# A gate product in seven block products instead of eight, in the last stage of a two-layer decoder trunk

## Chip, cores and metric

The kernel runs on one core of a Trainium2 chip. The time is the device time of one execution in microseconds (us). The median of three runs before the change is 1260.3 us (1259.97 to 1260.51). One further execution was profiled.

## What is computed

Two decoder layers over 512 tokens of width 1024, all in f32. Layer 0 mixes by sliding-window attention and a short convolution, layer 1 by chunked gated linear attention. Each layer then adds a gated MLP with a width-3 causal convolution, and a per-layer embedding. The change touches the end of layer 1: the down projection of its MLP, and the embedding that closes the kernel.

```python
for i in range(DEPTH):
    ...
    x = x + _conv_ffn(_rms_norm(x, ffn_norm[i]), ffn_w_up[i], ffn_conv_w[i], ffn_conv_b[i], ffn_w_down[i])
    x = x + _per_layer_embedding(x, p[i], ple_norm[i], ple_w_gate[i], ple_w_proj[i])
...
def _per_layer_embedding(x, p_i, norm, w_gate, w_proj):
    gate = jax.nn.sigmoid(_rms_norm(x, norm) @ w_gate)     # 512x1024 @ 1024x1024
    return gate * (p_i @ w_proj)                           # 512x256 @ 256x1024
```

## The kernel before

**Numbers.** The matmuls take operands of type fp32r. Every operand is split into a high part (ScalarE copies it to fp32r) and a low part (VectorE subtracts the high part from the original): `split` (L92) for activations, `cut` (L114) for weights. `mm3` (L149) then issues three matmuls for each block: high by high, high by low, low by high. So a product over a contraction of 1024 takes 8 blocks of 128 with 3 matmuls each, per 128 output rows and 512 output columns.

**Data.** The residual stream lies transposed in SBUF: eight tiles `xT[m]` of 128 channels by 512 tokens. The normalisation is deferred. `advance` (L228) multiplies a finished `xT[m]` by the gain, splits it, and adds its squares to `acc`; `end_norm` (L242) sums `acc` over the channels with four small matmuls, and `rsqrt` (L157) gives one factor per token, which is applied after the product.

**Weights.** A weight tile comes in by one DMA of up to 1 MB on SyncE's queue into one of two buffers `raw`, and is cut into halves that rotate through three buffers each of `wh` and `wl`. A DMA waits for the cuts of the tile before the last, a cut waits for the matmuls that read the same buffer three cuts earlier.

**The down projection** (`project`, L274) makes two output tiles m, m+1 at a time: 22 contraction blocks by 3 matmuls by 2 tiles, 132 matmuls a pair, four pairs. After each tile, `done` (L298) adds it to `xT[m]` and calls `advance`.

**The last stage** (`ple1`, L770) takes the eight split tiles as stationary operand, 128 tokens at a time, and the gate weights as moving operand, 512 columns at a time. First the left 512 columns for all four token tiles t, over all eight k, into four PSUM banks `ps`. Then p is transposed and split (`load_p`, L713), `back` (L787) transposes all of x back into eight tiles `xt`, and for each t `finish` (L798) closes the left half and the right half follows: 24 matmuls, then `finish` again. `finish` makes the product of p with the projection weights (six matmuls into `pj`), the sigmoid of the gate product (ScalarE), multiplies by `pj`, adds `xt` (both VectorE) and stores the result. The last right half is made in two pieces of 256 columns.

**Order.** A scheduler places the instructions of every engine at build time by priority and its own estimate of time, and assigns the waits between engines; at run time every engine goes through its list in order, and a waiting instruction holds up all that stand behind it. SyncE's list holds the DMAs. SBUF is given out by pools: the memory of the MLP's pool goes to the last stage's pool when the MLP's tiles have been read for the last time.

## Time and profile before

| | |
|---|---|
| median of 3 runs | 1260.3 us |
| the profiled execution: time | 1260.71 us |
| its span, first to last instruction | 1258.8 us |
| TensorE (PE) busy | 1244.9 us, 99% |
| VectorE (DVE) busy | 772.7 us, 61% |
| ScalarE (ACT) busy | 541.1 us, 43% |
| DMA, over the span | 117.42 MB, 93 GB/s |
| last stage, from its first matmul to the end of the span | 1194.48 to 1258.8 us |

All stretches of time below are in microseconds from the start of the span. PE is TensorE's matmul, PEld its weight load, POOL is GpSimd, SP is SyncE. A row of the timeline gives the start, the duration, the engine, the line of the kernel, the operation and its tiles; in brackets stands how long the engine had been idle before, and what ended that. Matmuls overlap: one of 512 columns is shown with 0.39 us, but the next starts 0.23 us later, and it is this step from start to start that counts. The same holds, by less, for VectorE and ScalarE.

### The profile page before, as it was taken

To read this page: it belongs to the slowest core of one execution; us is meant where nothing else is said; L and a number is where in the kernel's file an instruction comes from. 1 tells how busy PE (TensorE), PEld (TensorE's weight loads), DVE (VectorE), ACT (ScalarE), POOL (GpSimd) and SP (SyncE) were. 2 spreads that over 40 slices of the span, in tenths; PEclk is the share of its full clock that TensorE was granted. 3 is DMA by queue.
4 is the path that set the end of the run, shared out by engine and by line. 5 is a ranking of instruction groups with operands and counts; after the bars stand their busy time and mean duration, and the time that the engine had idled before them with its cause. 6 is when DMAs were issued, how large, how long until landed. Compare 5 with 4: busy or idle time off the path is not lost.

```text
span 1258.8 us, 14853 instructions
## 1 busy us (share of the span) xinstructions
PE 1244.9 (99%) x5851; PEld 1038.1 (82%) x5851; DVE 772.7 (61%) x1190; ACT 541.1 (43%) x831; POOL 54.1 (4%) x150
## 2 busy tenths in 40 slices
PE   7999999999999999999999999999999999999998
PEld 7777788888888888888989988888888888888887
DVE  6776566777777633346679765557777777433343
ACT  6456344444444422234563544335444444232341
POOL 2500000000000000000100000000000000000000
PEclk9999999999999999999999999999999999999999
DMA  6221232333332233223322222333222233222331
GB/s 212 73 76 55 79 99 93 100 101 101 100 100 92 76 111 99 92 74 101 109 89 67 68 68 67 100 100 102 98 88 86 98 100 101 92 92 93 108 107 61
DMA packets 110473, 117.42 MB, mean 93 GB/s; under 512 B 2712, under 2 KB 105682, under 8 KB 110404
## 3 DMA queue, kind: packets, MB, share of 16 engines
q1 hardware_dynamic: 108512, 114.83, 28.0%
q10 hardware_dynamic: 1332, 1.23, 0.3%
q8 instruction: 46, 0.75, 0.2%
q0 software_dynamic: 560, 0.42, 0.2%
q14 instruction: 23, 0.19, 0.0%
HBM read 114.37 MB, written 2.10 MB: 93 GB/s over the span
## 4 chain that ended last, share of the span: by engine, by line
PE 92%; DVE 3%; ACT 2%; issue 1%; POOL 1%; DMA 1%; SPq 0%; DVEq 0%; POOLq 0%; ACTq 0%
PE ps L153 28%; PE ps L155 28%; PE ps L154 28%; PE pa L492 1%; PE pa L1001 1%; DMA xin<-in_x_dram 1%; PE pa L1115 1%; PE pa L154 1%; DVE wl L134 1%; PE pa L153 1%; PE pa L155 1%; PE pa L538 1%; PE pa L1092 0%; POOL rq L163 0%; PE pa L1117 0%
## 5 line engine op out<-in xcount | busy, mean ns | idle before, releaser
L133 ACT ACTIVATE wh<-raw 128x1024 fp32r<-128x1024 f32 (+4 forms) x222 | 224.7, 1015 | 384.5 <-PE ps L154 319.4
L134 DVE TENSOR_TENSOR wl<-raw,wh 128x1024 fp32r<-128x1024 f32 (+4 forms) x222 | 258.6, 1167 | 184.0 <-ACT wh L133 182.9
L153 PE MATMUL ps<-a,wh 128*128 128x512 f32 x864 | 337.4, 390 | 0.0
L154 PE MATMUL ps<-a,wh 128*128 128x512 f32 x864 | 337.0, 390 | 0.0
L155 PE MATMUL ps<-a,wl 128*128 128x512 f32 x864 | 336.8, 390 | 0.0
L153 PEld LDWEIGHTS ps<-a,wh 128*128 128x128 f32 x864 | 162.5, 188 | 34.3 <-issue 0.7
L155 PEld LDWEIGHTS ps<-a,wl 128*128 128x128 f32 x864 | 162.5, 188 | 34.0 <-issue 0.2
L154 PEld LDWEIGHTS ps<-a,wh 128*128 128x128 f32 x864 | 162.5, 188 | 33.8 <-issue 0.3
L682 DVE SCALAR_TENSOR_TENSOR zt<-z,vfa,zt 128x512 f32<-128x512 f32 x176 | 131.4, 749 | 3.6 <-ACT zt L680 0.6
L153 PE MATMUL ps<-b,wh 128*128 128x512 f32 x320 | 126.3, 396 | 0.6 <-ACT b L97 0.5
L155 PE MATMUL ps<-b,wl 128*128 128x512 f32 x320 | 125.3, 392 | 0.0
L154 PE MATMUL ps<-b,wh 128*128 128x512 f32 x320 | 124.9, 391 | 0.0
L679 DVE TENSOR_TENSOR z<-ps,R 128x512 f32<-128x512 f32 x88 | 60.4, 688 | 74.7 <-PE ps L155 74.7
L153 PE MATMUL ps<-ah,wh 128*128 128x512 f32 x224 | 87.1, 389 | 0.0
L154 PE MATMUL ps<-al,wh 128*128 128x512 f32 x224 | 87.1, 389 | 0.0
L155 PE MATMUL ps<-ah,wl 128*128 128x512 f32 x224 | 87.1, 389 | 0.0
L680 ACT ACTIVATE zt<-z,vfb 128x512 f32<-128x512 f32 x88 | 70.9, 807 | 5.0 <-DVE z L679 3.3
L153 PEld LDWEIGHTS ps<-b,wh 128*128 128x128 f32 x320 | 60.0, 188 | 14.0 <-ACT b L97 1.3
L155 PEld LDWEIGHTS ps<-b,wl 128*128 128x128 f32 x320 | 60.1, 188 | 12.5
L154 PEld LDWEIGHTS ps<-b,wh 128*128 128x128 f32 x320 | 60.1, 188 | 12.2
L704 ACT ACTIVATE zt<-zt 128x512 f32<-128x512 f32 x44 | 27.8, 631 | 74.8 <-DVE zt L682 74.8
L299 DVE TENSOR_TENSOR xT<-xT,ps 128x512 f32<-128x512 f32 x32 | 22.0, 688 | 57.4 <-PE ps L155 57.4
(290 smaller groups left out, 1506.1 us busy)
## 6 DMA issues: line engine op xcount, KB each, us to landing
raw<-in_ffn_w_up_dram SPq DMA_DIRECT2D x44, 1024.0 KB, 5.0
raw<-in_ffn_w_down_dram SPq DMA_DIRECT2D x16, 1024.0 KB, 5.1
raw<-in_hy_w_in_dram SPq DMA_DIRECT2D x8, 1024.0 KB, 5.0
raw<-in_ple_w_gate_dram SPq DMA_DIRECT2D x8, 1024.0 KB, 5.0
raw<-in_gla_w_in_dram SPq DMA_DIRECT2D x8, 1024.0 KB, 5.3
raw<-in_ffn_w_down_dram SPq DMA_DIRECT2D x8, 768.0 KB, 4.3
raw<-in_gla_w_out_dram SPq DMA_DIRECT2D x4, 1024.0 KB, 5.0
raw<-in_gla_w_in_dram SPq DMA_DIRECT2D x4, 672.0 KB, 4.0
```

Of the source, the lines that this page charges most:

```text
L133: nc.scalar.activation(hv, v, AF.Copy)
L134: nc.vector.tensor_tensor(lv, v, hv.bitcast(F32), ALU.subtract)
L153: mm(out, lh, rh, start=start, stop=False)
L154: mm(out, lh, rl, start=False, stop=False)
L155: mm(out, ll, rh, start=False, stop=stop)
L299: self.nc.vector.tensor_tensor(self.xT[m], self.xT[m], ps, ALU.add)
L492: nc.tensor.matmul(pb[:, hh * 256 : hh * 256 + w], qTs[t][64 * g : 64 * g + 64, hq, :], kT[64 * g : 64 * g + 64, k0 : k0 + w], start=True, ...
L538: nc.tensor.transpose(pb[:, hh * P : (hh + 1) * P], s[:, 4 * g + hh, c * P : (c + 1) * P], self.ident)
L679: nc.vector.tensor_tensor(z[:, 2:], ps, R, ALU.mult)
L680: nc.scalar.activation(y, z[:, 2:], AF.Identity, scale=w2[:, f : f + 1], bias=bb[:, f : f + 1])
L682: nc.vector.scalar_tensor_tensor(out=y, in0=z[:, tap : tap + S], scalar=w[:, f : f + 1], in1=y, op0=ALU.mult, op1=ALU.add)
L704: nc.scalar.activation(y, y, AF.Gelu)
```

## The change

The gate product of the last stage is written as a product of 2 by 2 blocks: the contraction in even and odd blocks of 128 (e and o), the tokens in a first and a second half (1 and 2), the columns in a left and a right half. Eight block products become seven by Strassen's method in Winograd's form. With b11, b21 the left weights of the even and odd blocks and b12, b22 the right ones, the products are e1 b11, o1 b21, s1 (b12-b11), s2 (b22-b12+b11), s3 (b22-b12), s4 b22 and o2 (b21-b22+b12-b11), with s1 = e2+o2, s2 = s1-e1, s3 = e1-e2, s4 = o1-s2.

- The sums and differences of the activations are made where the down projection of layer 1 finishes a tile (`blocks`): for each pair of tiles VectorE makes s1 to s4 from the two gained tiles, and four operands (e1, o, s1 with s2, s3 with s4) are split, in place of two.
- Those of the weights are made in the last stage (`minus`), each in two VectorE instructions of 128x1024; the resulting blocks are cut like the others (`chunk`).
- Partial products that several results share are copied from PSUM to SBUF (`keep`, ScalarE) and added later (`summed`, VectorE), or stay in their bank and are added to.
- The gate weights arrive as four blocks of 1 MB: b11 and b21 into the two `raw` buffers, b12 and b22 (`rawx`) into the last stage's pool. The projection weights (512 KB) have one buffer `wjr` and are loaded three times. p comes in two halves on SyncE's queue, during the MLP, instead of one DMA on ScalarE's.
- The projection matmuls of a result (`proj`) now stand ahead of its gate product, and the transposes `back` are spread over the stage.
- In the whole stage the order of PE, VectorE and ScalarE is that of the source (`manual_schedule`); SyncE's is still the scheduler's. Each of the 7 products is 24 matmuls; the last one is ordered by result tile, its second tile in two pieces of 256 columns.

```diff
...
+    def blocks(self, m, gain, scratch):
+        nc = self.nc
+        H = S // 2
+        tags = ("a0", "a1") if m < 4 else ("b0", "b1")
+        gx = scratch()
+        nc.scalar.activation(gx, self.xT[m], AF.Copy, scale=gain[:, m : m + 1])
+        def parts(x):
+            w = x.shape[1]
+            h, l = self.pair(self.fp, *tags)
+            self.split((h[:, :w], l[:, :w]), x)
+            return lambda b, c: (h[:, b * H + c * P : b * H + (c + 1) * P], l[:, b * H + c * P : b * H + (c + 1) * P])
+        if m % 2 == 0:
+            self.even = gx
+            self.e1 = parts(gx[:, :H])
+        else:
+            e, o = self.even, gx
+            op = parts(o)
+            s12, s34 = scratch(), scratch()
+            nc.vector.tensor_tensor(s12[:, :H], e[:, H:], o[:, H:], ALU.add)
+            nc.vector.tensor_tensor(s12[:, H:], s12[:, :H], e[:, :H], ALU.subtract)
+            s12p = parts(s12)
+            nc.vector.tensor_tensor(s34[:, :H], e[:, :H], e[:, H:], ALU.subtract)
+            nc.vector.tensor_tensor(s34[:, H:], o[:, :H], s12[:, H:], ALU.subtract)
+            s34p = parts(s34)
+            e1 = self.e1
+            at = lambda f, b: lambda c: f(b, c)
+            self.forms.append(
+                dict(e1=at(e1, 0), o1=at(op, 0), o2=at(op, 1), s1=at(s12p, 0), s2=at(s12p, 1), s3=at(s34p, 0),
+                     s4=at(s34p, 1))
+            )
+        self.squares(m)
...
@@ -707,19 +752,37 @@
                     nc.vector.tensor_tensor(y, g, y, ALU.mult)
                     self.split(acts[f], y)
             self.begin_norm(("a0", "a1"))
-            self.project(self.rows(a["ffn_w_down"][i]), acts, ND, self.residual(next_gain))
+            done = self.residual(next_gain)
+            if i == 1:
+                self.forms = []
+                scratch = lambda: fp.tile([P, S], F32, tag="zt", name=self.nm("gx"), bufs=4)
+                def done(m, ps):
+                    nc.vector.tensor_tensor(self.xT[m], self.xT[m], ps, ALU.add)
+                    self.blocks(m, next_gain, scratch)
+            self.project(self.rows(a["ffn_w_down"][i]), acts, ND, done)
             self.end_norm()
-    def load_p(self, i, pool):
+    def p_halves(self, i):
+        src = self.a["p"][i, 0].rearrange("(t p) e -> p t e", p=P)
+        pin = [self.sp.tile([P, NT, P], F32, tag="R", name=self.nm("pin"), bufs=2) for _ in range(2)]
+        for e in range(2):
+            self.nc.sync.dma_start(pin[e], src[:, :, e * P : (e + 1) * P])
+        return pin
+    def load_p(self, i, pool, pin=None):
         nc = self.nc
-        pin = pool.tile([P, NT, 256], F32, name=self.nm("pin"))
-        nc.scalar.dma_start(pin, self.a["p"][i, 0].rearrange("(t p) e -> p t e", p=P))
+        if pin is None:
+            pi = pool.tile([P, NT, 256], F32, name=self.nm("pin"))
+            nc.scalar.dma_start(pi, self.a["p"][i, 0].rearrange("(t p) e -> p t e", p=P))
+            pin = [pi[:, :, e * P : (e + 1) * P] for e in range(2)]
         out = []
         for e in range(2):
             ps = self.pa()
             for t in range(NT):
-                nc.tensor.transpose(ps[:, t * P : (t + 1) * P], pin[:, t, e * P : (e + 1) * P], self.ident)
+                nc.tensor.transpose(ps[:, t * P : (t + 1) * P], pin[e][:, t, :], self.ident)
             hl = self.pair(pool, f"ph{e}", f"pl{e}")
             self.split(hl, ps)
             out.append(hl)
@@ -769,20 +832,66 @@
     def ple1(self):
         nc, a, tc = self.nc, self.a, self.tc
-        xg, r = self.xg, self.r
-        wg = a["ple_w_gate"][1].rearrange("(k p) n -> p k n", p=P)
+        r, forms = self.r, self.forms
+        wg = a["ple_w_gate"][1].rearrange("(j u p) n -> u p j n", p=P, u=2)
         wp = a["ple_w_proj"][1].rearrange("(k p) n -> p k n", p=P)
         sl = lambda hl, t: (hl[0][:, t * P : (t + 1) * P], hl[1][:, t * P : (t + 1) * P])
+        H, J = D // 2, ND // 2
         with tc.tile_pool(name="ple1", bufs=1) as fp:
-            def load(hf, pool, bufs):
-                ws = []
-                for k0 in (0, 4):
-                    raw = self.raw(4, 512)
-                    nc.sync.dma_start(raw, wg[:, k0 : k0 + 4, hf * 512 : hf * 512 + 512])
-                    ws.append(self.cut(raw, "a", pool, bufs))
-                return lambda k, c0, c1: ws[k // 4](k % 4, c0, c1)
+            def block(u, c, pool):
+                raw = self.raw(J, H) if pool is None else pool.tile([P, J, H], F32, tag="rawx", name=self.nm("rawx"), bufs=2)
+                nc.sync.dma_start(raw, wg[u, :, :, c * H : (c + 1) * H])
+                return raw
+            count = [0]
+            def chunk(src):
+                pool = (self.wp, fp)[count[0] % 6 // 3]
+                count[0] += 1
+                h, l = (pool.tile([P, 2, H], F32R, tag=g, name=self.nm(g), bufs=3) for g in ("wh", "wl"))
+                nc.scalar.activation(h, src, AF.Copy)
+                nc.vector.tensor_tensor(l, src, h.bitcast(F32), ALU.subtract)
+                return h, l
+            def chunks(raw):
+                return [chunk(raw[:, 2 * q : 2 * q + 2, :]) for q in range(2)]
+            def minus(out, x, y):
+                for q in range(2):
+                    c = slice(2 * q, 2 * q + 2)
+                    nc.vector.tensor_tensor(out[:, c, :], x[:, c, :], y[:, c, :], ALU.subtract)
+            def add(banks, form, ws, first=False, each=False):
+                both = ((0, H),)
+                order = [(j, i, both) for j in range(J) for i in range(2)]
+                if each:
+                    order = [(j, 0, both) for j in range(J)] + [
+                        (j, 1, (c,)) for c in ((0, H // 2), (H // 2, H)) for j in range(J)
+                    ]
+                mm = nc.tensor.matmul
+                for j, i, cs in order:
+                    lh, ll = forms[j][form](i)
+                    h, l = ws[j // 2]
+                    for c0, c1 in cs:
+                        rh, rl = h[:, j % 2, c0:c1], l[:, j % 2, c0:c1]
+                        o = banks[i][:, c0:c1]
+                        kw = dict(skip_group_check=True)
+                        mm(o, lh, rh, start=first and j == 0, stop=False, **kw)
+                        mm(o, lh, rl, start=False, stop=False, **kw)
+                        mm(o, ll, rh, start=False, stop=j == J - 1, **kw)
+            def keep(banks, tag):
+                out = []
+                for b in banks:
+                    k = self.sp.tile([P, S], F32, tag=tag, name=self.nm("keep"), bufs=2)
+                    nc.scalar.copy(k, b)
+                    out.append(k)
+                return out
             def back(hf, t):
@@ -791,40 +900,92 @@
                     nc.tensor.transpose(
                         pb[:, q * P : (q + 1) * P], self.xT[4 * hf + q][:, t * P : (t + 1) * P], self.ident
                     )
-                x = fp.tile([P, 512], F32, tag="xt", name=self.nm("xt"), bufs=8)
+                x = fp.tile([P, 512], F32, tag="xt", name=self.nm("xt"), bufs=4)
                 nc.scalar.copy(x, pb)
                 return x
-            def finish(hf, t, pg, x, w, c0=0, c1=512):
-                n = c1 - c0
+            def proj_w(hf):
+                raw = fp.tile([P, 2, H], F32, tag="wjr", name=self.nm("wjr"))
+                nc.sync.dma_start(raw, wp[:, :, hf * H : (hf + 1) * H])
+                return chunk(raw)
+            def proj(t, w):
                 pj = self.pa()
                 for k in range(2):
-                    self.mm3(pj[:, :n], sl(pT[k], t), w(k, c0, c1), start=k == 0, stop=k == 1)
-                s = fp.tile([P, 512], F32, tag="so", name=self.nm("so"), bufs=4)[:, :n]
-                nc.scalar.activation(s, pg, AF.Sigmoid, scale=r[:, t : t + 1])
-                nc.vector.tensor_tensor(s, s, pj[:, :n], ALU.mult)
+                    self.mm3(pj, sl(pT[k], t), (w[0][:, k, :], w[1][:, k, :]), start=k == 0, stop=k == 1)
+                return pj
+            def summed(g, kept):
+                s = fp.tile([P, H], F32, tag="so", name=self.nm("so"), bufs=3)
+                nc.vector.tensor_tensor(s, g, kept, ALU.add)
+                return s
+            def finish(hf, t, g, x, pj, s=None, c0=0, c1=H):
+                if s is None:
+                    s = fp.tile([P, H], F32, tag="so", name=self.nm("so"), bufs=3)
+                s = s[:, c0:c1]
+                nc.scalar.activation(s, g[:, c0:c1], AF.Sigmoid, scale=r[:, t : t + 1])
+                nc.vector.tensor_tensor(s, s, pj[:, c0:c1], ALU.mult)
                 nc.vector.tensor_tensor(s, s, x[:, c0:c1], ALU.add)
-                nc.sync.dma_start(self.out[0, t * P : (t + 1) * P, hf * 512 + c0 : hf * 512 + c1], s)
-
-            w = load(0, self.wp, 3)
-            pgs = [self.ps() for _ in range(NT)]
-            for k in range(ND):
-                for t in range(NT):
-                    self.mm3(pgs[t], sl(xg[k], t), w(k, 0, 512), start=k == 0, stop=k == ND - 1)
-            wj = self.weights(wp[:, :, :512], 2, 512, by="a")
-            pT = self.load_p(1, fp)
-            w = load(1, fp, 4)
-            wj1 = self.weights(wp[:, :, 512:], 2, 512, by="a")
-            x0 = [back(0, t) for t in range(NT)]
-            x1 = [back(1, t) for t in range(NT)]
-            for t in range(NT):
-                finish(0, t, pgs[t], x0[t], wj)
-                cuts = (0, 512) if t < NT - 1 else (0, 256, 512)
-                for c0, c1 in zip(cuts, cuts[1:]):
-                    pg = self.ps()[:, : c1 - c0]
-                    for k in range(ND):
-                        self.mm3(pg, sl(xg[k], t), w(k, c0, c1), start=k == 0, stop=k == ND - 1)
-                    finish(1, t, pg, x1[t], wj1, c0, c1)
+                nc.sync.dma_start(self.out[0, t * P : (t + 1) * P, hf * H + c0 : hf * H + c1], s)
+            b11 = block(0, 0, None)
+            w11 = chunks(b11)
+            b21 = block(1, 0, None)
+            w21 = chunks(b21)
+            b12 = block(0, 1, fp)
+            b22 = block(1, 1, fp)
+            pin = self.p_halves(1)
+            X, Y = [[self.ps() for _ in range(2)] for _ in range(2)]
+            ET = mybir.EngineType
+            with tc.manual_schedule(engines={ET.PE, ET.DVE, ET.Activation}):
+                add(X, "e1", w11, first=True)
+                ka = keep(X, "sq")
+                minus(b11, b12, b11)
+                wt1 = [chunk(b11[:, :2, :])]
+                pT = self.load_p(1, fp, pin)
+                wj = proj_w(0)
+                wt1.append(chunk(b11[:, 2:, :]))
+                xs = [back(0, t) for t in (0, 1)]
+                add(Y, "o1", w21, first=True)
+                pjs = [proj(t, wj) for t in (0, 1)]
+                ss = [summed(Y[t], ka[t]) for t in (0, 1)]
+                minus(b11, b22, b11)
+                wt2 = chunks(b11)
+                for t in (0, 1):
+                    finish(0, t, ss[t], xs[t], pjs[t], ss[t])
+                Q = [self.ps() for _ in range(2)]
+                add(Q, "s1", wt1, first=True)
+                minus(b12, b22, b12)
+                wt3 = [chunk(b12[:, :2, :])]
+                kd = keep(Q, "R")
+                wt3.append(chunk(b12[:, 2:, :]))
+                wj = proj_w(1)
+                add(X, "s2", wt2)
+                w22 = chunks(b22)
+                minus(b21, b21, b11)
+                kb = keep(X, "sq")
+                xs = [back(1, t) for t in (2, 3)]
+                pjs = [proj(t, wj) for t in (2, 3)]
+                add(X, "s3", wt3)
+                wt4 = [chunk(b21[:, :2, :])]
+                ss = [summed(X[t], kd[t]) for t in (0, 1)]
+                for t in (0, 1):
+                    finish(1, t + 2, ss[t], xs[t], pjs[t], ss[t])
+                xs = [back(1, t) for t in (0, 1)]
+                pjs = [proj(t, wj) for t in (0, 1)]
+                wt4.append(chunk(b21[:, 2:, :]))
+                wj = proj_w(0)
+                add(Q, "s4", w22)
+                ss = [summed(Q[t], kb[t]) for t in (0, 1)]
+                for t in (0, 1):
+                    finish(1, t, ss[t], xs[t], pjs[t], ss[t])
+                xs = [back(0, t) for t in (2, 3)]
+                pjs = [proj(t, wj) for t in (2, 3)]
+                add(X, "o2", wt4, each=True)
+                finish(0, 2, X[0], xs[0], pjs[0])
+                for c in ((0, H // 2), (H // 2, H)):
+                    finish(0, 3, X[1], xs[1], pjs[1], None, *c)
```

8 lines of the change are left out of this document (added).

## The prediction

> **What bounds the kernel now.** I read the profile's page first: the busy times, then the chain that ended last.
>
> ```profile
> span 1258.8 us, 14853 instructions
> PE 1244.9 (99%) x5851; PEld 1038.1 (82%) x5851; DVE 772.7 (61%) x1190; ACT 541.1 (43%) x831; POOL 54.1 (4%) x150
> ...
> PE 92%; DVE 3%; ACT 2%; issue 1%; POOL 1%; DMA 1%; SPq 0%; DVEq 0%; POOLq 0%; ACTq 0%
> ```
>
> TensorE never rests, so matmuls taken away are time gained, as long as nothing makes PE wait instead. Next I read the timeline where the last stage begins and where it ends.
>
> ```profile
> 1194.26 0.39 PE L155 MATMUL ps<-ah,wl 128*128 128x512 f32 x1
> 1194.48 0.39 PE L153 MATMUL ps<-wh,a 128*128 128x512 f32 x1
> 1194.50 1.06 ACT L133 ACTIVATE wh<-raw 128x1024 fp32r<-128x1024 f32 x1 [1.93 <-issue]
> 1194.68 0.69 DVE L299 TENSOR_TENSOR xT<-xT,ps 128x512 f32<-128x512 f32 x1 [0.73 <-PE ps L155]
> 1194.71 0.39 PE L154 MATMUL ps<-wl,a 128*128 128x512 f32 x1
> ...
> 1254.14 0.28 PE L155 MATMUL ps<-wh,a 128*128 128x256 f32 x1
> 1254.46 0.47 ACT L804 ACTIVATE so<-ps,rtok 128x256 f32<-128x256 f32 x1 [3.12 <-PE ps L155]
> 1254.86 0.28 PE L155 MATMUL pa<-wh,pl 128*128 128x256 f32 x1
> 1255.23 0.42 DVE L805 TENSOR_TENSOR so<-so,pa 128x256 f32<-128x256 f32 x1 [2.71 <-PE pa L155]
> 1255.69 0.42 DVE L806 TENSOR_TENSOR so<-so,xt 128x256 f32<-128x256 f32 x1
> ```
>
> A matmul of 512 columns starts every 0.227 us, and the stage follows the down projection without a gap. At the end the sigmoid hides under the last projection matmuls; two VectorE instructions and a store follow, and the span ends 2.7 us after the last of them.
>
> Then the prices, from the groups by line with forms kept apart, the DMA issues, and the stretch around 62 us, the only one where PE waited long.
>
> ```profile
> L134 DVE TENSOR_TENSOR wl<-raw,wh 128x1024 fp32r<-128x1024 f32 x186 | 227.3, 1224 | 108.3 <-ACT wh L133 107.2
> L133 ACT ACTIVATE wh<-raw 128x1024 fp32r<-128x1024 f32 x186 | 196.8, 1061 | 289.3 <-PE ps L154 238.1 <-issue 26.0 <-PE ps L155 20.2
> L98 DVE TENSOR_TENSOR al<-zt,ah 128x512 fp32r<-128x512 f32 x28 | 19.4, 693 | 19.5 <-ACT ah L97 19.5
> L795 ACT COPY xt<-pa 128x512 f32<-128x512 f32 x8 | 4.1, 611 | 0.0
> ...
> raw<-in_ple_w_gate_dram SPq DMA_DIRECT2D x8, 1024.0 KB, 5.0
> raw<-in_ple_w_proj_dram SPq DMA_DIRECT2D x2, 512.0 KB, 3.5
> ...
> 1212.00:1213.00 1.00, 1.00 (x6) 0.84 (x5) 0.00 (x0) 0.00 (x0) 0.00 (x0) 1.00 1.04 406
> ...
> 62.00:63.00 1.00, 0.00 (x0) 0.00 (x0) 0.86 (x4) 0.98 (x2) 0.55 (x1) 1.00 0.76 196
> 63.00:64.00 1.00, 0.00 (x0) 0.00 (x0) 1.00 (x3) 0.50 (x1) 1.00 (x1) 1.00 1.08 375
> 66.00:67.00 1.00, 1.00 (x3) 0.81 (x4) 1.00 (x11) 0.00 (x0) 0.00 (x0) 0.50 0.12 24
> ```
>
> Started back to back, an instruction costs a little less than it lasts: three cuts in 3.50 us make steps of 1.14 us on VectorE, three in 2.96 us 0.95 us on ScalarE; 512 columns step by 0.64 and about 0.5, 256 columns on VectorE by 0.38. A full DMA queue moves about 406 GB/s (last number of the row at 1212).
>
> **The change part by part.** The order of instructions of the changed kernel and its waits are known, its times are not. I laid that order out from 1194.48 on with the steps above and 0.05 us for each hand-over between engines. Laid out so, the old stage ends 0.2 us early, and everything ahead of it keeps its time.
>
> *Removed.* 8 products become 7: 24 matmuls of 0.227 us, 5.44 us. There were 60 pieces of 256 columns at 0.120 us, now 24; the 36 fewer, at 0.007 us above half a full step, give 0.24. A wait of 0.2 us ahead of the old `back` goes. Together -5.9.
>
> *Activation sums in the down projection.* Per pair of tiles VectorE now has four weight cuts of 1.22 and two of 0.96, two additions into xT, two of squares and three splits of 0.69, one split and four sums of 0.42: 13.7 us; ScalarE some 11. A pair lasts 132 x 0.227 = 29.9 us on PE, so this is covered, and no weight cut comes late. Without that cover the price would be the extra 2.6 us per pair. The halves of p on SyncE's queue go out between weight DMAs whose own buffers come free later. Nothing.
>
> *Only the last tile, m=7, is not covered.* VectorE: addition 1194.7, cut of b21 from 1195.6 (ScalarE's half comes first), then four sums, two splits and the squares, in line. The squares end at 1199.2, and the four matmuls of `end_norm`, after 20 of the first product, start 0.2 us late. The last split ends at 1201.0. **+0.2**
>
> *First stall: the loads of b12, b22 and `wjr`.* The memory of b12 is that of the MLP's pool, whose last reader is this last split. So the DMA of b12 goes out at 1201.0, where the old kernel had both `raw` buffers filling ahead; b22 and `wjr` stand behind it on SyncE. b12 lands 5.0 us later (row), at 1206.0; 1 MB more at 406 GB/s is 2.6, 0.5 MB 1.3: `wjr` lands at 1209.9. From below, 2.6 MB at that rate behind the row's latency cannot land before 1209.7. From above, the three one after the other (5.0+5.0+3.5) land at 1214.5. I take 1209.9, since in the old stage the 0.5 MB load issued during the 1 MB one kept the queue at 300 to 406 GB/s. Behind b12 stand the two subtractions and the cuts of b12-b11, the splits of p, and then the cut of `wjr`, in line on both engines: ScalarE ends its half at 1211.0, VectorE its half at 1212.3. PE finishes o1 b21 at 1208.1 and its next matmuls are the projection. It waits 2.9 us for the high part, does one matmul, and waits 1.05 for the low part. **+4.0**
>
> *Second stall.* From 1212.3 on VectorE has hardly a break before it reaches the second `wjr`: one cut, two subtractions, two cuts, two subtractions and three cuts (10 x 1.14), six additions and multiplications of two results (6 x 0.68), and 1.6 of waiting for ScalarE (the table load of 1.28 ahead of the first sigmoid; two copies and two cuts ahead of a cut): 17.1, so the low part is ready at 1229.4. PE, after s1 and s2 (48 x 0.227) and 8 transposes of 0.109, is there at 1226.6. **+2.6**
>
> *Third and fourth.* Ahead of s4 and of o2, `pj` needs a PSUM bank that a result of the product just ended must read first: addition 0.69, sigmoid 0.63, multiplication 0.69, with hand-overs and the rest of its bank's last matmul 2.4 us; the other bank's three matmuls and 8 transposes cover 0.68+0.87. **+0.8 twice**
>
> *Tail.* Both 256-column pieces of the last result lie in one bank, and the wait for it names its last matmul. So both sigmoids and four VectorE instructions follow the last matmul, and no projection hides them: from its start 0.28, sigmoid 0.42, then 0.45, 0.38, 0.45 and 0.42 with 0.1 of hand-overs, 2.5, against 1.25 before (1254.86 to 1256.11). **+1.3**
>
> Sum: -5.9+0.2+4.0+2.6+1.6+1.3 = +3.8. The profiled execution took 1260.71 (span 1258.8 and 1.9 around it), 0.4 above the median, so 1264.5 against it and **1264.1** against the median of 1260.3.
>
> **The rivals.** (1) *The waits are hidden, and the change gains.* For it: PE saves 5.7 whatever else happens. If ScalarE and VectorE get through the projection's cuts before 1208.1 and 1226.6, only the tail remains: 1260.3-5.9+1.3 = 1255.7. It turns faster once the stalls add up to less than 4.6. Against it: b12 waits for m=7's split, and even with loads that take no time, the same layout leaves +1.4. (2) *Loads hidden, engines not:* that +1.4, 1261.7, within 0.2%. (3) *The loads do not overlap:* `wjr` at 1214.5 in place of 1209.9 and b22 late too, +6.1 in the layout: 1266.4. For it: each row of 5.0 us was measured with little else in the queue. (4) *The clock falls in a stall.* At 62.0 to 64.2 us PE had nothing to do, and at 66 the granted clock was 0.50; the timeline has matmuls of 512 columns start at 66.33, 66.76 and 67.19 there, 0.43 apart instead of 0.227, for some 3.4 us (64.9 to 68.3), which loses 1.7. The first stall is 4.2 us with one matmul in it. If the clock falls there, PE arrives up to 1.7 late at the second stall, which is 2.6 long, and that swallows it. It is paid in full only if the second stall triggers it alone: 1264.1+1.7 = 1265.8. The Trainium skill, "TensorE: Matmul & The Clock Gate", Part 1, has the clock halved after about one idle window of 3.4 us, a window that runs free; by that rule the first stall can trigger it and the second cannot. The row at 62 us, 2.2 us idle, shows that less is enough.
>
> That the change does not do what it says is no case: PE's order has 168 gate matmuls' worth where there were 192.
>
> **How the numbers follow.** A measurement of this kernel tells 0.2% (2.5 us) from no change. My forecast has 0.62, and 1262.2 to 1266 as its own range, from a 5% error of all VectorE and ScalarE steps (-1.2, +1.1) and slower hand-overs (+0.4). Rival 1 has 0.07, rival 2 0.11, rival 3 and 4 0.10 each. Faster is rival 1: 0.07. Same is rival 2 and the low tenth of the forecast: 0.17. Slower is the rest: 0.76. The range runs from below rival 2 to above rival 3: 1261.0 to 1267.2.
>
> **What would show it.** Right: in the last stage PE idle for about 4 us near 1208, ended by ScalarE's and VectorE's cut of `wjr`, and again for 2 to 3 us near 1227; the b12 DMA issued near 1201; a tail of 4 VectorE instructions; down projection unchanged. A granted clock of 0.5 after 1210 would show rival 4. Wrong: `wjr` landing before 1208, or PE waits in the stage that sum to less than 4 us.

## The result, and the profile after

The changed kernel takes 1264.73 us (median of 6 runs, 1264.22 to 1265.26), the kernel before 1260.4 (6 runs, 1259.97 to 1261.09). The ratio is 1.0032 with a 95% interval of 1.0022 to 1.0042: slower by 4.3 us. The forecast was 1264.1 with a range of 1261.0 to 1267.2. The profiled execution took 1264.94 us.

The page of the changed kernel, its span and busy times and then the chain that ended last:

```profile
span 1263.2 us, 14856 instructions
PE 1242.6 (98%) x5809; PEld 1034.1 (82%) x5809; DVE 802.7 (64%) x1235; ACT 559.4 (44%) x860; POOL 54.3 (4%) x150
...
PE 93%; DVE 2%; issue 1%; DMA 1%; ACT 1%; POOL 1%; SPq 0%; DVEq 0%; POOLq 0%
```

PE's busy time fell by 2.3 us and the span grew by 4.4, so about 6.7 us in which PE did nothing have come in. The view of PE's waits in the last stage (engine, tile and line, what was waited for: us in total, times, longest) names them:

```profile
PE pa L153 <- ACT wh L855: 2.8, 1, 2.8
PE pa L154 <- DVE wl L856: 1.6, 2, 0.9
PE pa L153 <- DVE so L928: 1.4, 2, 0.7
```

The first two are waits for the cut of the projection weights (`wh`, `wl`), the third for VectorE's work on earlier results (`so`). The timeline of the changed kernel shows each in its place:

```profile
1200.86 0.92 SPq L846 DMA_DIRECT2D rawx<-in_ple_w_gate_dram  x2
1201.83 10.71 SPq L909 DMA_DIRECT2D wjr<-in_ple_w_proj_dram  x2
...
1205.98 2.36 DVE L865 TENSOR_TENSOR raw<-rawx,raw 128x1024 f32<-128x1024 f32 x2 [2.12 <-DMA rawx<-in_ple_w_gate_dram]
...
1207.79 0.39 PE L886 MATMUL ps<-wh,b 128*128 128x512 f32 x1
1209.84 1.06 ACT L855 ACTIVATE wh<-wjr 128x1024 fp32r<-128x1024 f32 x1 [0.56 <-DMA wjr<-in_ple_w_proj_dram]
1210.92 1.23 DVE L856 TENSOR_TENSOR wl<-wjr,wh 128x1024 fp32r<-128x1024 f32 x1 [0.17 <-ACT wh L855]
1210.95 0.50 PE L153 MATMUL pa<-wh,ph 128*128 128x512 f32 x1 [2.77 <-ACT wh L855]
1212.21 0.59 PE L154 MATMUL pa<-wl,ph 128*128 128x512 f32 x1 [0.76 <-DVE wl L856]
...
1228.11 0.47 PE L153 MATMUL pa<-wh,ph 128*128 128x512 f32 x1
1228.17 1.22 DVE L856 TENSOR_TENSOR wl<-wjr,wh 128x1024 fp32r<-128x1024 f32 x1
1229.45 0.50 PE L154 MATMUL pa<-wl,ph 128*128 128x512 f32 x1 [0.86 <-DVE wl L856]
...
1239.25 0.50 PE L153 MATMUL pa<-wh,ph 128*128 128x512 f32 x1 [0.70 <-DVE so L928]
...
1249.29 0.50 PE L153 MATMUL pa<-wh,ph 128*128 128x512 f32 x1 [0.70 <-DVE so L928]
```

SyncE issues the DMAs of b12 and b22 at 1200.9 and that of `wjr` behind them (the row of `wjr` takes its second load, some 10 us later, in with the first). VectorE begins to subtract when b12 has landed, at 1205.98; ScalarE begins to cut `wjr` at 1209.84. PE starts its last matmul of o1 b21 at 1207.79, the next at 1210.95 and the one after at 1212.21. With a step of 0.227 that is 2.93 and 1.03 lost, 3.96 in all. The second stall has 1.11 (1228.11 to 1229.45), the third and the fourth 0.86 and 0.87 beyond the eight transposes ahead of them.

The windows of the changed kernel by microsecond (after the length come the busy times of PE, PEld, DVE, ACT and POOL, then PE's granted clock) show what followed the first stall:

```profile
1212.00:1213.00 1.00, 0.79 (x2) 0.63 (x3) 1.00 (x2) 0.80 (x2) 0.00 (x0) 0.74 0.00 0
1213.00:1214.00 1.00, 1.00 (x4) 0.79 (x3) 1.00 (x3) 0.00 (x0) 0.00 (x0) 0.50 0.55 139
1214.00:1215.00 1.00, 1.00 (x4) 0.81 (x3) 1.00 (x2) 0.00 (x0) 0.00 (x0) 0.50 0.90 342
1215.00:1216.00 1.00, 1.00 (x4) 0.76 (x4) 1.00 (x2) 0.35 (x1) 0.00 (x0) 0.56 0.11 43
1216.00:1217.00 1.00, 1.00 (x6) 0.83 (x5) 1.00 (x2) 0.87 (x2) 0.00 (x0) 1.00 0.00 0
```

Four matmuls are at work in a microsecond where the clock is 0.50, six where it is 1.00 (those that began earlier are counted in). If the clock is either 0.50 or 1.00, the rows make 0.52 + 1 + 1 + 0.88 = 3.4 us at half clock. Nine steps, from 1212.21 to 1215.96, took 3.75 in place of 2.04: 1.71 lost.

The tail of the changed kernel, in its timeline:

```profile
1257.61 0.28 PE L886 MATMUL ps<-wh,b 128*128 128x256 f32 x1
1257.93 0.84 ACT L927 ACTIVATE so<-ps,rtok 128x256 f32<-128x256 f32 x2 [2.18 <-PE ps L886]
1258.43 0.42 DVE L928 TENSOR_TENSOR so<-so,pa 128x256 f32<-128x256 f32 x1 [1.24 <-ACT so L927]
...
1259.68 0.42 DVE L929 TENSOR_TENSOR so<-so,xt 128x256 f32<-128x256 f32 x1
```

Both sigmoids follow PE's last matmul, and VectorE ends 2.49 after its start; before it was 1.25. The span then ends 3.1 later; before it was 2.7.

In the profiled executions the last stage begins between 1193.3 and 1196.0, though nothing that matters was changed ahead of it: at 32 to 33 us of the span some are already 1.0 apart. So profiled executions are compared by the length of the stage, from its first gate matmul. All in us:

| kernel | first to last matmul | then to VectorE's end | then to the span's end | sum | median | kernel before on the same chip | ratio, 95% |
|---|---|---|---|---|---|---|---|
| before | 60.38 | 1.25 | 2.7 | 64.3 | 1260.4 | | |
| changed | 63.28 | 2.49 | 3.1 | 68.9 | 1264.73 | 1260.4 | 1.0022 to 1.0042 |
| e1 order left to the scheduler | 57.07 | 2.27 | 3.2 | 62.5 | 1258.86 | 1260.46 | 0.9979 to 0.9997 |
| e2 scratch in its own pool | 60.88 | 2.49 | 3.1 | 66.5 | 1262.29 | 1260.46 | 1.0005 to 1.0023 |
| e3 projection last | 63.33 | 1.33 | 3.0 | 67.7 | 1264.73 | 1260.46 | 1.0019 to 1.0042 |
| e4 first stall filled | 63.42 | 2.49 | 3.0 | 68.9 | 1266.87 | 1260.46 | 1.0033 to 1.0060 |
| e5 `wjr` first | 64.44 | 2.49 | 3.0 | 70.0 | 1265.70 | 1260.62 | 1.0031 to 1.0059 |
| e6 both stalls filled | 63.14 | 2.49 | 3.0 | 68.6 | 1264.92 | 1260.62 | 1.0023 to 1.0049 |
| e7 = e1 + e2 | 55.01 | 2.29 | 3.2 | 60.5 | 1256.46 | 1260.62 | 0.9956 to 0.9979 |
| e8 all, order free | 54.45 | 1.32 | 3.0 | 58.8 | 1254.89 | 1260.62 | 0.9942 to 0.9969 |
| e9 all, order fixed | 55.32 | 1.32 | 3.1 | 59.7 | 1255.72 | 1260.53 | 0.9945 to 0.9972 |
| e10 `wjr` and its cut first | 63.75 | 2.49 | 3.1 | 69.4 | 1264.85 | 1260.53 | 1.0019 to 1.0042 |

The seven products are kept in all of them but the first.

### The profile page after: what moved, and what is told of

The parts are those of the page before. It is cut to its first block, busy times and chain, and to the rows that moved or that the text cites. A ratio compares the mean times of both kernels' runs of the same rounds, so it can differ in the third digit from the quotient of the medians.

```text
span 1263.2 us, 14856 instructions
## 1 busy us (share of the span) xinstructions
PE 1242.6 (98%) x5809; PEld 1034.1 (82%) x5809; DVE 802.7 (64%) x1235; ACT 559.4 (44%) x860; POOL 54.3 (4%) x150
## 4 chain that ended last, share of the span: by engine, by line
PE 93%; DVE 2%; issue 1%; DMA 1%; ACT 1%; POOL 1%; SPq 0%; DVEq 0%; POOLq 0%
PE ps L153 28%; PE ps L154 28%; PE ps L155 28%; PE pa L1162 1%; PE ps L884 1%; PE ps L885 1%; PE pa L537 1%; PE ps L886 1%; PE pa L154 1%; DMA wjr<-in_ple_w_proj_dram 1%; PE pa L153 1%; PE pa L155 1%; PE pa L1276 1%; DMA xin<-in_x_dram 1%; PE pa L583 1%
## 5 line engine op out<-in xcount | busy, mean ns | idle before, releaser
L133 ACT ACTIVATE wh<-raw 128x1024 fp32r<-128x1024 f32 (+4 forms) x212 | 214.4, 1013 | 352.6 <-PE ps L154 306.3
L134 DVE TENSOR_TENSOR wl<-raw,wh 128x1024 fp32r<-128x1024 f32 (+4 forms) x212 | 246.5, 1164 | 160.7 <-ACT wh L133 159.6
L97 ACT ACTIVATE ah<-zt 128x512 fp32r<-128x512 f32 x28 | 17.7, 632 | 77.3 <-DVE zt L752 77.3
```

What stands on the lines that cost most here:

```text
L97: nc.scalar.activation(h, src, AF.Copy)
L133: nc.scalar.activation(hv, v, AF.Copy)
L134: nc.vector.tensor_tensor(lv, v, hv.bitcast(F32), ALU.subtract)
```

## The experiments

### Is it the order? (e1)

```diff
-            with tc.manual_schedule(engines={ET.PE, ET.DVE, ET.Activation}):
+            if True:
```

> The seven products stay, the last stage's order of instructions on TensorE, VectorE and ScalarE is left to the scheduler instead of being fixed. Theory (the stalls come of the order: the projection's matmuls stand ahead of work that could run, and the loads alone don't hold TensorE): the scheduler's order, laid out with the same steps, lets TensorE take s1 times b12-b11 ahead of the first projection; the waits left are 0.2 at end_norm, 1.0 and 1.0 near 1209 to 1210, and 0.2 in all later; the tail of 2.5 stays. That is 6.2 us less than the changed kernel's 1264.7: 1258.5, and 1.9 under the kernel before. The clock stays at full speed after the shorter waits. Rival (the late loads of b12, b22 and wjr set the first stall whatever the order): the first stall stays 4 us, the half clock too, and at most the 1.6 of the third and fourth goes: 1263 or more.

It took 1258.86 us, 1.6 less than before and 5.9 less than the changed kernel; the stage is 6.3 shorter. Its view of PE's waits in the stage has only these:

```profile
PE ps L884 <- DVE so L920: 0.8, 1, 0.8
PE ps L885 <- DVE wl L856: 0.6, 1, 0.6
```

The scheduler put s1's product (L884, L885) where the fixed order has the first projection. It needs b12-b11, which is cut before `wjr`. The first of its two waits ends with VectorE's sum of an earlier result, the second with the cut of b12-b11. The loads were no earlier (b12 and b22 issued at 1201.1), and yet of the first stall's 4.0 only 1.8 is left (1208.05 to 1209.28 and on to 1210.32, each less a step); the half clock and the second to fourth stall are gone. The rival is out: late loads did not hold PE whatever the order. So one line of the change, which fixes this order, decides its sign, though by little: the ratio to the kernel before is 0.9988, its interval ends at 0.9997.

### Is it the late loads? (e2)

```diff
-                y = fp.tile([P, S], F32, tag="zt", name=self.nm("zt"), bufs=4)
+                y = (self.gp if i else fp).tile([P, S], F32, tag="zt", name=self.nm("zt"), bufs=4)
...
-                scratch = lambda: fp.tile([P, S], F32, tag="zt", name=self.nm("gx"), bufs=4)
+                scratch = lambda: self.gp.tile([P, S], F32, tag="zt", name=self.nm("gx"), bufs=4)
...
-        self.ffn(1, self.g_ple[1])
-        self.ple1()
+        with self.tc.tile_pool(name="gx", bufs=1) as self.gp:
+            self.ffn(1, self.g_ple[1])
+            self.ple1()
```

(The edit also takes the tiles `xt` from the new pool.)

> The order stays fixed; the scratch tiles of the activation sums (and the tiles xt) move from the MLP's pool and the last stage's pool into a pool of their own that outlives both, so that the memory of b12 comes free with the down projection's last matmul and not with the last split of m=7. Theory: b12's DMA goes out near 1194.5 in place of 1200.9, wjr lands near 1204, its cut is done before TensorE has finished o1 b21, and the first stall falls from 4.0 to 0.1; with no idle stretch there the clock stays full, the second stall is 2.6 again, third, fourth and tail stay. 1264.7 - 3.7 = 1261.0. Rival (VectorE and ScalarE, whose work stands in line, set the first stall, not the loads): the stall stays above 2 us and the time within 1.5 of 1264.7. If the second stall, 2.6 us, halves the clock by itself, 1.7 is added: 1262.7.

It took 1262.29, between the 1261.0 and the 1262.7 of the two cases of the theory. Its timeline, and its windows behind it:

```profile
1195.18 0.92 SPq L846 DMA_DIRECT2D rawx<-in_ple_w_gate_dram  x2
...
1224.59 0.50 PE L153 MATMUL pa<-wh,ph 128*128 128x512 f32 x1 [1.12 <-ACT wh L855]
1226.04 0.50 PE L154 MATMUL pa<-wl,ph 128*128 128x512 f32 x1 [0.95 <-DVE wl L856]
```

```profile
1227.00:1228.00 1.00, 1.00 (x4) 0.82 (x4) 1.00 (x2) 1.00 (x3) 0.00 (x0) 0.67 0.69 180
1228.00:1229.00 1.00, 1.00 (x4) 0.72 (x4) 1.00 (x2) 0.36 (x1) 0.00 (x0) 0.50 0.91 334
1229.00:1230.00 1.00, 1.00 (x4) 0.81 (x3) 1.00 (x2) 0.52 (x1) 0.00 (x0) 0.50 0.07 27
1230.00:1231.00 1.00, 1.00 (x5) 0.78 (x4) 0.95 (x2) 0.54 (x1) 0.00 (x0) 0.63 0.00 0
```

The loads go out 5.7 earlier (6.3 counted from the stage's start, 1194.94 here) and the first stall is gone: PE's timeline has no wait with a releaser before 1224.59. The second stall, 1.28 beyond the transposes and 1.22 over a step, stands where VectorE's line put it, and here it halved the clock by itself: nine steps from 1227.30 to 1230.94 took 3.64 in place of 2.04, 1.6 lost. The stage is 2.4 shorter; without the half clock it would be 4.0.

### Which queue? (e5 and e10)

e5 moves one load:

```diff
...
+            wj0 = proj_raw(0)
             b12 = block(0, 1, fp)
...
-                wj = proj_w(0)
+                wj = chunk(wj0)
```

(`proj_raw` is the load in `proj_w` without its cut.)

> Only the place of one load changes: the first load of the projection weights (wjr, 0.5 MB) goes out ahead of b12 and b22 instead of behind them; memory, and the order on TensorE, VectorE and ScalarE, stay. Theory (the cut of wjr stands in line behind the subtractions that wait for b12, so an earlier wjr is of no use and b12 comes 1.3 later): VectorE's subtractions begin near 1207.2 in place of 1206.0, the first stall grows by 1.1 to 5.1, all behind it moves by that: 1264.7 + 1.1 = 1265.8, plus 1.7 at most if the clock falls for a second window. Rival (the stall is wjr's landing, third in the queue): wjr lands near 1204.5, the projection starts on time at 1208.1, and the first stall goes: 1261 to 1262.

It took 1265.70, and the stage grew by 1.1. In its timeline:

```profile
1200.37 0.37 SPq L909 DMA_DIRECT2D wjr<-in_ple_w_proj_dram  x1
1200.79 1.01 SPq L846 DMA_DIRECT2D rawx<-in_ple_w_gate_dram  x2
...
1206.84 2.36 DVE L865 TENSOR_TENSOR raw<-rawx,raw 128x1024 f32<-128x1024 f32 x2 [3.46 <-DMA rawx<-in_ple_w_gate_dram]
...
1211.16 0.77 PE L153 MATMUL pa<-wh,ph 128*128 128x512 f32 x1 [3.48 <-ACT wh L855]
1212.80 0.79 PE L154 MATMUL pa<-wl,ph 128*128 128x512 f32 x1 [0.87 <-DVE wl L856]
```

The earlier `wjr` lands about 3.6 us after its issue, at some 1204, but ScalarE cuts it only at 1210.02, behind the work on b12, and b12 comes later: counted from the stage's start VectorE's subtractions begin 1.35 later (1206.84 less 1193.84, against 1205.98 less 1194.33). PE's wait is named after the cut of `wjr`, but `wjr`'s landing was not its cause.

e10 adds the same step on the engines:

```diff
-                minus(b11, b12, b11)
-                wt1 = [chunk(b11[:, :2, :])]
                 pT = self.load_p(1, fp, pin)
                 wj = chunk(wj0)
+                minus(b11, b12, b11)
+                wt1 = [chunk(b11[:, :2, :])]
```

> The load of wjr goes first, and its cut and p's splits also stand ahead of the subtractions that wait for b12; memory stays. Theory (queue and engines' order must both change): the projection starts on time at 1208.1, TensorE then waits 1.9 for b12-b11 near 1211 to 1212.6, the second stall is 3.4 with one matmul in it, the others stay: 1264.7 - 1.3 = 1263.4 at a full clock; the second stall halves the clock at least in some executions, which adds 1.7 there: 1263.4 to 1265.1. Rival (the first stall is b12's late landing alone, whatever is moved ahead of it): 1265.7, as with the load alone.

It took 1264.85. Its view of PE's waits:

```profile
PE ps L884 <- DVE so L923: 2.0, 1, 2.0
PE pa L153 <- ACT wh L855: 1.9, 1, 1.9
PE pa L153 <- DVE so L931: 1.4, 2, 0.7
PE pa L154 <- DVE wl L856: 0.9, 1, 0.9
```

The first projection starts on time, and PE waits ahead of s1's product instead: 2.1 over a step (1210.86 to 1213.21) in place of 4.0. The second stall, now 1.9 and 0.9, came with a half clock behind it (matmuls 0.43 apart from 1229.77 to 1232.75). That would use up the gain, and the median has none of it; but the profiled execution, at 1265.76, was the slowest of the six, and the clock in the others is not traced. So the first stall has no single cause. It needs b12 late, and work ahead of the projection's cuts that waits for b12, and no other product for PE; e2, e10 and e1 each take one of these away.

### What does the half clock cost? (e4 and e6)

```diff
...
                 add(Y, "o1", w21, first=True)
+                for _ in range(11):
+                    nc.tensor.matmul(X[0], zeros, w21[1][0][:, 1, :], start=False, stop=False, skip_group_check=True)
                 pjs = [proj(t, wj) for t in (0, 1)]
```

(`zeros` is a tile of zeros of 128 by 128, made ahead of the stage.)

> Eleven matmuls of a tile of zeros with 512 columns of w21 are added between o1 b21 and the first projection, where TensorE waits anyway; they add zeros to a bank, 11 x 0.227 = 2.5 us, and take nothing from the work behind. Theory (the half clock after the first stall costs 1.7 there, and the second stall swallows it, since that one ends when VectorE has cut the second wjr): the granted clock stays 1.00 through 1212 to 1216, TensorE comes 1.7 earlier to the second stall and waits 2.6 there in place of 1.1, total unchanged, 1264.7 within 0.4. Rival (the half clock is paid in full): 1263.0. If the clock falls in spite of the filler, idle time is not what lowers it.

The profiled execution is as the theory has it. Its windows, of the stretch that was at half clock in the changed kernel, and of the second stall and what follows:

```profile
1211.00:1214.00 3.00, 2.74 (x12) 2.31 (x13) 3.00 (x5) 0.85 (x2) 0.00 (x0) 1.00 0.49 158
1227.00:1229.00 2.00, 0.99 (x3) 0.64 (x4) 2.00 (x3) 2.00 (x3) 0.00 (x0) 1.00 0.00 0
1229.00:1232.00 3.00, 3.00 (x15) 2.47 (x14) 3.00 (x4) 1.88 (x5) 0.00 (x0) 1.00 0.51 173
```

The clock stays full, the second stall is 1.4 and 1.2 long, the 2.6 of the forecast, and the stage is 68.9, as long as the changed kernel's. But the times did not fit the forecast: two of 1264.0 to 1264.3 and three of 1266.9 to 1267.1, median 1266.87. If the second stall alone halves the clock in some executions, as it did in e2, the upper three are explained but for about 1 us. e6 fills the second stall too:

```diff
                 xs = [back(1, t) for t in (2, 3)]
+                for _ in range(11):
+                    nc.tensor.matmul(Q[0], zeros, wt2[1][0][:, 1, :], start=False, stop=False, skip_group_check=True)
                 pjs = [proj(t, wj) for t in (2, 3)]
```

> The run with filled first stall, and eleven more matmuls of zeros ahead of the second projection, where the second stall is. Theory (that run's times in two groups, 1264.0 to 1264.3 and 1266.9 to 1267.1, come of the granted clock: with the first stall filled the second, 2.6 us, halves the clock by itself in some executions, depending on where it falls in the clock's window, and behind the second stall nothing swallows it): with both filled the clock stays full in the whole stage, the upper group is gone, all runs within 1263.5 to 1265.5, median 1264.5. Rival (the two groups come from the 1 us by which the executions differ in the first 35 us of the kernel, or from the filler itself): the spread stays 2 to 3 us, median 1264 to 1267.

Five runs from 1264.3 to 1265.5, median 1264.92: the upper group is gone. Its windows for the whole stage:

```profile
1194.00:1258.00 64.00, 61.62 (x301) 50.51 (x299) 46.40 (x56) 32.10 (x45) 1.38 (x1) 1.00 0.22 83
```

With a full clock throughout it takes as long as the changed kernel with 3.4 us of half clock. So in the changed kernel the half clock costs nothing: it uses up time that PE would spend waiting for the second `wjr`. None of the upper runs of e4 has a trace, so that the clock made them is inferred from e6, e2 and e10. The mean granted clock of the whole execution points the same way, 0.997 in the upper three and 0.998 and 0.999 in the lower two, but weakly: 3.4 us at half clock are 0.0013 of the span, and two of e6's five runs have 0.997 as well.

### The tail (e3)

```diff
...
-                pjs = [proj(t, wj) for t in (2, 3)]
-                add(X, "o2", wt4, each=True)
+                pjs = [proj(2, wj)]
+                add(X, "o2", wt4, each=0)
                 finish(0, 2, X[0], xs[0], pjs[0])
+                add(X, "o2", wt4, each=1)
                 for c in ((0, H // 2), (H // 2, H)):
-                    finish(0, 3, X[1], xs[1], pjs[1], None, *c)
+                    finish(0, 3, X[1], xs[1], proj(3, wj, *c), None, *c)
```

(`each` now names the one result tile that `add` makes, and `proj` takes a range of columns.)

> Only the end is changed: the projection of the last token tile comes after the last gate product instead of ahead of o2, in two pieces of 256 columns. Theory (the tail is long because both sigmoids wait for TensorE's last matmul): the sigmoids run beside the twelve projection matmuls, two VectorE instructions follow the last matmul, from its start to VectorE's end 1.25 in place of 2.49; total 1264.7 - 1.3 = 1263.4. The two last stores then go out further apart, and if their closeness made the end 0.37 longer than before the change, another 0.3 goes: 1263.1. Rival (the stores' completion sets the end whatever the engines do): within 0.4 of 1264.7.

The tail did what the theory expected, by the timeline of e3:

```profile
1255.65 0.84 ACT L926 ACTIVATE so<-ps,rtok 128x256 f32<-128x256 f32 x2 [2.03 <-PE ps L883]
...
1256.76 0.28 PE L155 MATMUL pa<-wh,pl 128*128 128x256 f32 x1
1257.22 0.41 DVE L927 TENSOR_TENSOR so<-so,pa 128x256 f32<-128x256 f32 x1
1257.67 0.42 DVE L928 TENSOR_TENSOR so<-so,xt 128x256 f32<-128x256 f32 x1
```

The sigmoids are over before the last matmul, and VectorE ends 1.33 after its start, 1.16 less; the profiled stage is 1.2 shorter. But the median, 1264.73, did not move: it is what the rival forecast, and the theory's 1263.4 was missed. The rival's reason is out, since the span ended 3.0 after VectorE in e3 as well, 1.2 earlier in the stage. The gain is missing in four of the six runs, of 1264.4 to 1265.3; the other two took 1262.7 and 1262.9. It is not shown that the clock takes it: the profiled execution is the one of 1262.92, and it had 6.8 us at half clock behind the first stall (0.55, 0.50, 0.50 and 0.74 in windows of 2 us from 1210 on), twice the 3.4 of the changed kernel. Its stage also began 0.9 earlier than the changed kernel's, so part of its lead lies ahead of the stage. What the four runs lose stays open. The same tail is in e8 and e9.

### All together (e7, e8, e9)

> Two edits together: the scratch tiles in a pool of their own, and the last stage's order left to the scheduler. Theory (early loads and the scheduler's order remove the same first stall; what the loads add is the 1.9 that the scheduler's order still waits near 1209): waits of 0.2 at end_norm and 0.1 in all later, 2.0 less than without the fixed order alone, 1258.9 - 2.0 = 1256.9, 3.5 under the kernel before. Rival (the two gains add up, 5.9 by the one, 2.4 by the other): 1256.5 if the half clock of the run with the pool of its own is counted, 1254.8 if not. Another rival (the memory doesn't matter once the order is free): 1258.9.

1256.46. The time does not decide between the theory's 1256.9 and the rival's 1256.5, which counts e2's half clock. The profile does: its PE has no wait with a releaser left in the stage, and a full clock, so there is no half clock to count. Its stage is 8.4 shorter than the changed kernel's; e1's 6.3 and e2's 4.0 without the half clock would add up to 10.3. It is 2.0 shorter than e1's, as the theory had it. Both remedies take away the same first stall, and the gains do not add up.

e8 adds e3's tail and moves three kinds of steps in the text: the closing of the first two results, the `keep` of s2's, and the projections. The scheduler takes the text's order as its priority:

```diff
...
-                for t in (0, 1):
-                    finish(0, t, ss[t], xs[t], pjs[t], ss[t])
...
-                wt3 = [chunk(b12[:, :2, :])]
                 kd = keep(Q, "R")
-                wt3.append(chunk(b12[:, 2:, :]))
+                wt3 = chunks(b12)
+                for t in (0, 1):
+                    finish(0, t, ss[t], xs[t], pjs[t], ss[t])
...
                 add(X, "s2", wt2)
+                kb = keep(X, "sq")
                 w22 = chunks(b22)
                 minus(b21, b21, b11)
-                kb = keep(X, "sq")
                 xs = [back(1, t) for t in (2, 3)]
-                pjs = [proj(t, wj) for t in (2, 3)]
                 add(X, "s3", wt3)
+                pjs = [proj(t, wj) for t in (2, 3)]
...
-                pjs = [proj(t, wj) for t in (0, 1)]
                 wt4.append(chunk(b21[:, 2:, :]))
-                wj = proj_w(0)
+                wr, wj = wj, proj_w(0)
                 add(Q, "s4", w22)
+                pjs = [proj(t, wr) for t in (0, 1)]
...
-                pjs = [proj(2, wj)]
                 add(X, "o2", wt4, each=0)
+                pjs = [proj(2, wj)]
```

> The seven products with all remedies: scratch tiles in a pool of their own, projections placed behind the products whose results must free their banks (behind s3, behind s4, and within o2), the last one behind the last gate product in two pieces, the first two results closed behind the cuts of s3's weights, and the order left to the scheduler with this text's order as its priority. Theory: no wait above 0.25 is left in the stage and the tail is 1.25, so that the saving of 5.9 is kept but for 0.2 at end_norm and 0.3 at the stores: 1260.4 - 5.4 = 1255.0. Rival (a wait that the layout does not show takes their place): 1257 or more.

1254.89 us, ratio 0.9956 (0.9942 to 0.9969): 5.7 under the kernel before, 9.8 under the changed one, which ran on another chip. Its windows, in one row for nearly the whole stage:

```profile
1194.00:1249.00 55.00, 55.00 (x273) 46.10 (x271) 45.20 (x57) 32.84 (x46) 3.05 (x1) 1.00 0.28 101
```

PE is busy for all of the 55 us, at full clock. e9 is the same text with the order fixed again:

> The kernel with all remedies, but with the order of TensorE, VectorE and ScalarE fixed as its text has it. Theory (not the fixing costs, but the order that was fixed: the projections ahead of the products, and loads behind the last split): waits of 0.4 at end_norm, 0.1 and 0.25 in the stage, 0.6 more than with the scheduler: 1255.5, 5 under the kernel before. Rival (a fixed order costs by itself, since what runs late cannot be passed by): 1258 or more.

1255.72, with one named wait of 0.3 left. That is 0.8 more than e8, measured on another chip; the two ratios to the kernel before, 0.9959 and 0.9956, can't be told apart. So it is not the fixing that costs, but the order that was fixed.

### The end of the span (e11 and e12)

```diff
...
-                nc.sync.dma_start(self.out[0, t * P : (t + 1) * P, hf * H + c0 : hf * H + c1], s)
+                q = nc.scalar if c0 else nc.sync
+                q.dma_start(self.out[0, t * P : (t + 1) * P, hf * H + c0 : hf * H + c1], s)
```

> The kernel with all remedies (order left to the scheduler), with the last 128 KB store issued by ScalarE's queue instead of SyncE's. Asked: why the span ends 3.0 to 3.2 after the last VectorE instruction in every kernel with seven products, and 2.7 after it in the kernel before. Theory (the store ahead, 128 KB issued 0.8 earlier in the same queue, holds up the last one): 2.7 after VectorE's end. Rival (it is not the queue): 3.0 to 3.2.

```diff
...
-                s = s[:, c0:c1]
+                whole, s = s, s[:, c0:c1]
...
-                nc.sync.dma_start(self.out[0, t * P : (t + 1) * P, hf * H + c0 : hf * H + c1], s)
+                if c1 == H:
+                    nc.sync.dma_start(self.out[0, t * P : (t + 1) * P, hf * H : (hf + 1) * H], whole)
```

> The same kernel, with one store of 256 KB for both pieces of the last result in place of two of 128 KB. Theory (two stores close together cost 0.35): with no store ahead within 3 us, the larger one takes 0.3 more for its 128 KB at 406 GB/s and ends 2.7 + 0.3 = 3.0 after VectorE's last instruction. Rival (the closeness has no part): 3.0 + 0.3 = 3.3 or more.

The span ended 3.1 after VectorE's last instruction in e11 (1253.0 less 1249.93) and 2.9 in e12 (1253.4 less 1250.47); the times are 1254.81 and 1255.02. It is not the queue. One large store ended near the theory's 3.0 and not at the rival's 3.3. The rows of DMA issues bear out the 0.3 for its size: the last store lands 1.7 after its issue where it has 128 KB (changed kernel, e8, e11), and 2.0 where it has 256 KB (e12). But they put the difference elsewhere than the theory does. Two stores close together land no later than 1.7; it is from the last landing to the span's end that 1.3 to 1.4 pass in those three, and 0.9 in e12. The old profile shows no landing of its last store. So why the kernel before ended 2.7 after its last instruction stays open.

## Why the prediction was right

Its mechanism was right: PE lost its time at the places that the prediction named, for the reasons that it gave. Its sum, 3.8, stands against 4.4 in the span and 4.3 in the median:

| term | predicted | measured |
|---|---|---|
| removed work | -5.9 | -5.7 (8.6 of waits and half clock, less the 2.9 by which first to last matmul grew) |
| sums hidden in the down projection | 0 | -0.15 (the stage begins at 1194.33, before at 1194.48) |
| `end_norm` behind m=7 | +0.2 | +0.1 (0.93 from the matmul ahead of its four to the one behind, less a step, against 0.81) |
| first stall | +4.0 | +3.96 |
| second stall | +2.6 | +2.8 (1.11, and 1.71 at half clock ahead of it) |
| third and fourth | +0.8 each | +0.86, +0.87 |
| tail | +1.3 | +1.24 |
| stores | none | +0.4 |

The measured removed work is a remainder, so the right column adds up to the span's 4.4 by construction. The stage's start differs by less than profiled executions scatter. The other rows are read one by one from the timelines. The largest errors, 0.4 for the stores and 0.2 each for the removed work and the second stall, all make the kernel slower, so the sum is not right by errors that cancel.

- *First stall.* Subtractions were forecast from 1206.0, `wjr` landed at 1209.9, low part ready at 1212.3; the trace has 1205.98, 1209.84 and 1212.15. That b12 waits for the memory of the scratch tiles was shown by e2, where that tie was cut.
- *Second stall.* VectorE's line between the two cuts of `wjr` was forecast at 17.1 and took 17.24 (1212.15 to 1229.39), with the waits for ScalarE that were forecast at 1.6 (0.81, 0.69 and 0.1). PE cannot pass the end of this line, so what PE loses ahead of it, idle or at half speed, costs nothing more until it exceeds the stall.
- *Rival 4*, the clock, came true in the first stall, as the text of the prediction had it for that case, and was swallowed; e4 and e6 show that. The row at 62 us, 2.2 us idle, was the row to go by: the stall had 2.8 us without a matmul, then one, then 0.8. The Trainium skill, "TensorE: Matmul & The Clock Gate", Part 1, says that the window runs free and that the number of slow matmuls of the same kernel varies from run to run. The 3.4 us at half clock agree with the length of its window; e4's two groups would fit the variation, but their clock is not traced. Its sentence that the clock falls after at least one idle window is not borne out to the letter: in e2 the second stall, 2.5 us with a matmul in it, was enough, which by that rule it could not be.
- *Rival 2*, loads hidden and engines not, was priced at 1261.7; e2 is nearly that case and took 1262.29. That the two are so close is in part luck: e2's profile has 1.6 of half clock that the price did not have, and without it its stage would be 0.5 longer than before the change, where the price was 1.4.
- *Rival 1*, everything hidden, was 1255.7 with the tail left as it was. e7 has that, at 1256.46: the saving was real, and the order and one pool kept it from showing.
- *Tail.* Both sigmoids waited for the last matmul of the bank that the two pieces share, as forecast. e3 and e8 shortened the tail by moving other matmuls behind the bank's last; pieces in two banks were not tried. The Trainium skill, "PSUM — Partial Sum Buffer", Terms, calls it an error when TensorE writes a bank that ScalarE reads at the same time; the changed kernel's tail agrees in so far as the sigmoid of a piece that was done 1.4 us earlier (1256.17 against 1257.61) starts only after the last matmul of its bank.
- *What failed* is small. The stores (0.4) were taken over from the old profile, and the cause of the difference was not found. And the removed work came out 0.2 smaller: the matmuls alone are 5.68, and the old wait of 0.19 ahead of `back` did go, but the first matmul behind a wait or behind transposes takes a step of 0.32 to 0.34 in place of 0.23 (1229.45 to 1229.79), and the changed kernel has five such at full clock where the old stage had three.

What the prediction did not ask is how much of the loss lay in the order alone. It took the fixed order as given and priced its waits one by one, and so did not see that with the same prices the scheduler's order comes out ahead of the kernel before, as e1's forecast of 1258.5 then did.

## What to carry to other kernels

Work saved on the engine that bounds a kernel is worth what the operands' makers can follow: lay out the other engines' lines and the loads up to each first use, and ask which memory a load waits for, since a short-lived tile can keep a pool's memory from the next stage until its last reader, as the scratch tiles did here. A wait is named after the instruction that ended it; e5 shows that moving that one's input earlier can make it longer. Before work on the loads, look for other ready work to put in front of the wait, and if an order is fixed by hand, compare it with the scheduler's.

## What the runs showed of the hardware that was not expected

- The granted clock fell to 0.50 for 3.4 us, in e3 for 6.8, behind idle stretches shorter than 3.4 us: 2.8 us, one matmul and 0.8 (changed kernel); 1.1 and 0.95, one matmul between them (e2). It fell when PE was at work again, in e2 some 1.3 us later (1226.04, and 1227.34 by the 0.67 of that window), so that no wait in the profile names the loss. In e4's profile nearly the same second stall, 1.26 and 0.96, left the clock at 1.00, and so did e1's 0.84 and 0.57. Where nothing behind it waits, it costs 1.6 to 1.7, four tenths of this change's whole effect. That executions of one kernel differ in it is inferred from e4's times and not traced.
- Each of the seven-product kernels ends 2.9 to 3.2 after VectorE's last instruction, the kernel before 2.7. The last store takes 1.7 of it from issue to landing, and 2.0 in e12 with twice the size. The cause of the difference was not found.
- Executions of the same instructions reach the same place up to 1 us apart by 33 us of the span (33.10 in the changed kernel's profile, 32.08 and 32.15 in those of e3 and e4, at GpSimd's first normalisation).
